# Squares for the RMS norms summed over the channel tiles on VectorE, in place of TensorE

## The chip, the cores and the metric
The kernel runs on one core of a Trainium2 chip. The metric is the device time of one execution, in microseconds (us). Engines are named as the profile names them: PE is TensorE (PEld its weight loads), DVE is VectorE, ACT is ScalarE, POOL is GpSimd, SP is the engine that issues the DMAs.

## What is computed
Two layers of a hybrid block over 512 latent and 256 context tokens of 1024 channels: RMS norm and modulation, one input projection for three branches (attention, a state-space model, a conformer convolution), a gated merge of the branches, an output projection and a gated residual; then a last RMS norm. The norm is what the change touches:

```python
def rmsnorm(x, w):
    xf = x.astype(jnp.float32)
    y = xf * lax.rsqrt(jnp.mean(xf * xf, axis=-1, keepdims=True) + EPS)
    return (y * w.astype(jnp.float32)).astype(x.dtype)
...
    h = rmsnorm(x, norm_w) * (1.0 + scale) + shift
    hc = rmsnorm(xc, norm_w) * (1.0 + scale_c) + shift_c
...
    x_new = x + gate * out
    return x_new, xc + gate_c * out_c
```

The mean is over the 1024 channels of a token. The last layer makes no new context, and its `x_new` goes through the final norm.

## The kernel before
**Layout.** Activations lie channel-major: 8 channel tiles `k` of 128 channels on the partitions, tokens along the free dimension (0 to 511 latent, 512 to 767 context). A sum over channels thus is a sum over 8 tiles and over 128 partitions. Products of float32 are made of three products of shorter parts (`hh`/`hl` or `yh`/`yl` of the data, `whi`/`wlo` of the weights), in `mm_cm_steps` (L161, the product on L175). `wload` (L141) streams weights: a DMA into `raw` (3 buffers), the high part on ACT (L156), the low part on DVE (L157), each with 5 buffers.

**The norm.** `class Rms` (L253) works on a span of tokens in three steps.
- `add` (L261), for each channel tile: ACT squares it into `sq` (L263); then `add_up` has PE multiply `sq` by a 128x32 block of ones (L268), tile `k` into the 32 PSUM partitions of group `k % 4`. After 8 tiles the PSUM tile `ps_ss` holds four partial sums on partitions 0, 32, 64, 96 (and copies beside them). A span over 512 tokens has two such tiles.
- `steps` (L278): ACT copies `ps_ss` to `sspart` (L282); a first yield; PE multiplies `sspart` by `sel4`, which picks the four partitions, 128 tokens to a product (L286), so that tokens come onto the partitions; DVE scales (L288); POOL takes the power −0.5 (L290); a second yield; DVE makes diagonals `dg` (L297), PE spreads them over the partitions with a block of ones into `ps_rb` (L298), ACT copies to `rb` (L299).
- The users: `affine_in` makes `ht` (DVE, L354), `hh` (ACT, L356), `hl` (DVE, L357) of each channel tile; the final norm makes `ot` (DVE, L1138), which goes out by DMA.

Rows of up to 512 tokens (`sq`, `sspart`, `dg`, `rb`, `ht`, and the residual tiles `xr`) share a pool of 7 buffers (tag W2), longer ones a pool of 3 (tag F).

**Where norms stand.** (1) At the start, over all 768 tokens at once, while the modulation weights (`wm`) stream in and PE makes the modulation (`mod_tiles` L221: products L229, ACT copy `part` L232, second step L237, DVE L238); the first products of the conformer, `ps_u`, follow as `hh` comes tile by tile. (2) At the layer boundary, first over the latent span, then over the context span (L382 to L386), while the last tiles of layer 0's output projection `ps_o` run; then come `ps_u` and `ps_g` of layer 1. (3) In the tail, over two parts of 256 latent tokens: 5 output tiles for both parts, then the last 3 for part 1, then the same 3 for part 2, with part 1's norm put between part 2's products. There the order of PE, DVE and ACT is as written (L1155), and `NORM_PACE` says after which pieces of four products (`PIECE` columns) the norm moves on by one yield:

```python
        for ct, w in zip(kept, ws):
            for j, _ in enumerate(out_steps(ct, parts[1:], w)):
                if j == 2:
                    add_up()
                if next(pace):
                    next(first, None)
            add_up = norm_add(1, ct)
```

An output tile (`out_steps`, L1098) fetches `xr` (L1102), makes 24 products per span (`ps_o`, in one of two PSUM banks), and DVE forms `xnew` from `ps_o` and `xr` (L1106), which frees the bank. Apart from the tail, and from PE's order inside a layer, which is as written too, a scheduler orders the instructions of each engine; every engine runs its queue in order.

Of the kernel before, what the change touches and what calls it, by code (L numbers as in the profile page):

```python
# [12 lines left out]
ALU = mybir.AluOpType  # L13
# [28 lines left out]
# How the tensor engine's work is spread, per layer.  # L42
GATES_EARLY = (0, 2)             # tiles of the attention's gate made before the conformer's gate
CONV_GATE_FIRST = (0, 4)         # turns of the conformer's gate before its layer norm
AHEAD_TILES = (1, 3, 5, 7)       # tiles of the last merge whose gates are made ahead of it,
AHEAD = ((2, 3), (3, 4))         # so many by the end of the SSD, and by the end of attention
SSD_END = ((2, 0.5, 2), (2, 0.5, 0))  # turns kept for the SSD's end, its transposes, the first q and k
ATTN_SPARE = (13, 9)             # turns of attention beyond those of its tiles
CTX_TURN = 1.75                  # weight of a turn of a context tile, which has fewer of them
PIECE = 1024                     # columns per piece of woven work  # L50
MOD_LAG = 5120                   # columns between a modulation product and its second step
OUT_FIRST = 3                    # output tiles that take both of their spans at once
KEPT = 3                         # last output tiles, whose weights stay for the second part
NORM_PACE = (0, 0, 1, 0, 0, 1, 0, 0, 0)  # pieces of the last products after which the norm moves on, at first
# [3 lines left out]
def hybrid_kernel(ctx, tc, xT, cc, consts, rope, mod_params, params, fnw, w_mod, w_cm, w_q, w_kvd, w_z,  # L58
# [48 lines left out]
    # ---- inputs that the start waits for  # L107
# [15 lines left out]
    sel, sel4 = cst[:, 384:386], cst[:, 386:388]  # L123
# [8 lines left out]
    def rsqrt(v, scale):  # L132
        """v := (v * scale + eps) ** -0.5"""
        G.tensor_scalar(out=v, in0=v, scalar1=scale, scalar2=EPS, op0=ALU.mult, op1=ALU.add)
        e = nhalf
        for _ in range(len(v.shape) - 2):
            e = e.unsqueeze(1)
        G.tensor_tensor(out=v, in0=v, in1=e.to_broadcast(list(v.shape)), op=ALU.pow)

    def wload(src, nk, ncol, prio=TOP, keep=None):  # L140
        """Stream nk k-tiles of ncol columns, split each into two float32r parts (in keep, where given)."""  # L141
        per, half = {P: (8, 4), 256: (4, 2)}.get(ncol, (2, 2))
        res = []
        with tc.high_priority(offset=prio):
            for k0 in range(0, nk, per):
                n = min(per, nk - k0)
                raw = wp.tile([P, n, ncol], F32, tag="raw", name="raw")
                nc.sync.dma_start(raw, src[:, k0:k0 + n, :])
                for u0 in range(0, n, half):
                    m = min(half, n - u0)  # L150
                    if keep is None:
                        hi = wp.tile([P, m, ncol], F32R, tag="whi", name="whi", bufs=5)
                        lo = wp.tile([P, m, ncol], F32R, tag="wlo", name="wlo", bufs=5)
                    else:
                        hi, lo = (keep[:, i, k0 + u0:k0 + u0 + m, :] for i in range(2))
                    S.activation(hi, raw[:, u0:u0 + m, :], AF.Copy)  # L156
                    V.tensor_tensor(out=lo, in0=raw[:, u0:u0 + m, :], in1=f(hi), op=ALU.subtract)  # L157
                    res += [(hi[:, i, :], lo[:, i, :]) for i in range(m)]
        return res

    def mm_cm_steps(w, xh, xl, ntok, evac, name, col=slice(None), psum=None, late=False, piece=PIECE):  # L161
        """sum_k w[k].T @ x[k] in two parts each, per group of tokens; evac(ps, a, b) takes it.

        Yields the columns streamed, piece by piece, so that the caller can put other work between.
        """
        nk = len(w)
        spans = ntok if isinstance(ntok, tuple) else [(a, min(ntok, a + 512)) for a in range(0, ntok, 512)]
        for a, b in spans:
            ps = (psum or pjt)(name)
            done = 0  # L170
            order = [(k, w[k][i], x) for k in range(nk) for i, x in ((0, xh), (0, xl), (1, xh))]
            if late:
                order.sort(key=lambda o: o[2] is xl)
            for n, (k, st, mv) in enumerate(order):
                T.matmul(ps[:, :b - a], st[:, col], mv(k)[:, a:b], start=(n == 0), stop=(n == len(order) - 1))  # L175
                done += b - a
                if done >= piece and n < len(order) - 1:
                    yield done
                    done = 0
            evac(ps[:, :b - a], a, b)  # L180
            yield done
# [8 lines left out]
    class Weave:  # L190
        """Work of total columns that is emitted piece by piece, spread over n turns of another part."""
# [29 lines left out]
    def mod_tiles(li, mod, m0, tiles, psum=pot):  # L221
        """Columns m0.. of silu(c) @ w_mod + b_mod, channels on partitions; tiles: [P, KD, P] each."""
# [30 lines left out]
    class Rms:  # L253
        """1 / rms over the channels of tokens t0..t1, on every partition; add takes one channel tile."""

        def __init__(self, t0, t1, psum=pot):
            self.t0, self.n, self.psum = t0, t1 - t0, psum
            self.groups = [(a, min(self.n, a + 512)) for a in range(0, self.n, 512)]
            self.pss = [psum("ps_ss") for _ in self.groups]

        def add(self, k, x):  # L261
            sq = row(self.n, "sq")
            S.activation(sq, x[:, self.t0:self.t0 + self.n], AF.Square)  # L263
            g = k % 4

            def add_up():
                for ps, (a, b) in zip(self.pss, self.groups):
                    T.matmul(ps[32 * g:32 * g + 32, :b - a], ones[:, 0:32], sq[:, a:b], start=(k < 4), stop=(k >= 4),  # L268
                             tile_position=(0, 32 * g))
# [8 lines left out]
        def steps(self):  # L278
            n, nt = self.n, self.n // P
            part = row(n, "sspart")  # L280
            for ps, (a, b) in zip(self.pss, self.groups):
                S.activation(part[:, a:b], ps[:, :b - a], AF.Copy)  # L282
            yield
            ps2 = self.psum("ps_ss2")
            for i in range(nt):
                T.matmul(ps2[:, 2 * i:2 * i + 2], part[:, tok(i)], sel4, start=True, stop=True)  # L286
# [31 lines left out]
    for li in range(2):  # L318
# [7 lines left out]
        # ---- per-layer tables  # L326
# [15 lines left out]
        # the attention's scale, a power of two, goes into the weights of the q norm  # L342
# [3 lines left out]
        # ---- norm and modulation  # L346
# [44 lines left out]
        # ---- conformer: gated linear unit, into zero-padded rows that share their pads  # L391
# [7 lines left out]
        # its depthwise convolution is emitted tap by tap  # L399
# [20 lines left out]
        for ct in range(4):  # L420
            # the first products start on channels as the norm hands them over, in banks of their own
# [27 lines left out]
        # ---- k, v, dt (token-major)  # L449
# [13 lines left out]
        # ---- dt = softplus(.), decays  # L463
# [22 lines left out]
        # ---- SSD inputs  # L486
# [51 lines left out]
        # ---- z (token-major)  # L538
# [14 lines left out]
        # ---- decays of the chunks  # L553
# [12 lines left out]
        # ---- q (token-major), kept in DRAM until attention; the conformer's layer norm between its tiles  # L566
# [47 lines left out]
        def gate_steps(c0, c1):  # L614
            """The attention's gate, twice its silu, kept in DRAM until attention's end."""
# [20 lines left out]
        # ---- gated merge of one branch  # L636
        yh, yl = [], []

        def then(fn, steps):
            """The steps, with fn after some of them."""  # L640
# [16 lines left out]
        def ahead_steps(a, b):  # L657
            """Gates of the last merge, kept in DRAM until it."""
# [54 lines left out]
        # ---- SSD states: st[0:4] backward into each latent chunk, st[4:6] forward, rolling  # L713
# [22 lines left out]
        class Chunk:  # L736
            """Output of chunk c, gated and normalised, written over xt[:, c]."""
# [14 lines left out]
            def decay(self, g):  # L752
                """The chunk's own weights, of four heads."""
# [58 lines left out]
        # ---- q / k: norm over the head, rope, transposed and stacked parts  # L812
        def qk_prep(src, nh, t0, nt, wo, cw, sw, dst, dup):
            """src [P, nt, nh*64] token-major (token tiles t0..), into their columns of dst."""
# [47 lines left out]
        class Pipe:  # L862
            """Preparations of q and k, each in three steps, the steps of consecutive ones side by side."""
# [33 lines left out]
        # ---- the SSD's steps, one chunk's decays ahead of another's products  # L897
# [75 lines left out]
        def scores(hp2, qi, fill):  # L973
            """exp(scores - max) over its sum, of two heads for one tile of queries."""
# [79 lines left out]
        # ---- attention, with the merge of the SSD's branch between its steps  # L1054
# [40 lines left out]
        # ---- output projection and residual  # L1095
# [20 lines left out]
        if not last:  # L1116
            # the last tiles' second span comes behind everything else
# [7 lines left out]
    # ---- the last tiles, and the norm, one part of the tokens after another  # L1125
# [29 lines left out]
    # the first part's norm goes between the second part's products  # L1155
# [107 lines left out]
```

## Time and profile before

| what | value |
|---|---|
| runs of the kernel | median 1512.54 us of 3 (1509.86 to 1516.24) |
| span of the profiled execution, first to last instruction | 1508.5 us |
| own time of the profiled execution | not given beside its span |
| PE busy | 1475.4 us (98%) |
| DVE, ACT, POOL busy | 1020.7 (68%), 724.6 (48%), 80.2 us (5%) |
| chain that ended last | PE 93%, DMA 2%, ACT 2%, DVE 1% |
| mean granted TensorE clock | 0.997 |

Busy is the time in which an engine ran instructions; the chain is followed back from the last instruction, at each step to what released it. The median of the runs lies 4.0 us above the profiled span.

### The profile page before, as it was taken

The page shows a single profiled execution, that of the slowest core. Times are in us where ns is not written, and L with a number is a line of the kernel's source. Part 1 is how long each engine was busy: PE and PEld are TensorE (multiplying, and loading weights), DVE is VectorE, ACT ScalarE, POOL GpSimd, SP SyncE. Part 2 cuts the span into 40 slices and gives each one's busy share as a digit, 9 for nine tenths or more (in the row PEclk, how much of TensorE's full clock was granted, in tenths as well). Part 3 has the DMA queues.
Part 4 walks back from the last instruction along what each step waited for, and adds up shares of the span by engine and source line. Part 5 has one row for each costly group of instructions (what it writes and reads, how often), then busy time and mean ns, then how long its engine had stood idle before and what let it go on. Part 6 is the DMA issues. An engine that isn't in the chain of part 4 may idle for free.

```text
span 1508.5 us, 25204 instructions
## 1 busy us (share of the span) xinstructions
PE 1475.4 (98%) x9812; PEld 1257.7 (83%) x9812; DVE 1020.7 (68%) x1876; ACT 724.6 (48%) x1630; POOL 80.2 (5%) x177
## 2 busy tenths in 40 slices
PE   7999999999999999999999999999999999999997
PEld 5898899988888888888888867989988887888886
DVE  3689999666568676555443357899977788665642
ACT  5324543465445575655322254355464657665431
POOL 0000010100003010000000000001010121000000
PEclk9999999999999999999999999999999999999998
DMA  9222333223333323333742422223423242223532
GB/s 377 70 68 92 112 127 100 69 74 105 106 117 128 122 69 123 109 109 107 244 156 91 162 87 80 73 70 113 143 74 112 95 161 71 96 94 105 182 109 74
DMA packets 69687, 172.59 MB, mean 114 GB/s; under 512 B 7872, under 2 KB 24384, under 8 KB 69568
## 3 DMA queue, kind: packets, MB, share of 16 engines
q1 hardware_dynamic: 69568, 170.98, 33.7%
q8 instruction: 77, 1.26, 0.3%
q14 instruction: 42, 0.34, 0.1%
HBM read 143.43 MB, written 27.53 MB: 113 GB/s over the span
## 4 chain that ended last, share of the span: by engine, by line
PE 93%; DMA 2%; ACT 2%; DVE 1%; issue 1%; SPq 0%; POOL 0%; POOLq 0%; DVEq 0%; ACTq 0%
PE ps_gm L175 22%; PE ps_br L175 11%; PE ps_xbc L175 9%; PE ps_o L175 7%; PE ps_u L175 4%; PE ps_gcv L175 4%; PE ps_g L175 4%; PE po_v L1043 3%; PE ps_ga L175 3%; PE pt_p L1029 3%; PE ps_l L983 2%; PE ps_mod L229 2%; PE ps_z L216 1%; PE ps_q L216 1%; PE ps_q L217 1%; PE ps_z L217 1%
## 5 line engine op out<-in xcount | busy, mean ns | idle before, releaser
L156 ACT ACTIVATE whi<-raw 128x512 fp32r<-128x512 f32 (+1 forms) x316 | 199.2, 633 | 291.3 <-PE ps_gm L175 63.9
L157 DVE TENSOR_TENSOR wlo<-raw,whi 128x512 fp32r<-128x512 f32 (+1 forms) x316 | 216.7, 689 | 171.3 <-ACT whi L156 163.1
L175 PE MATMUL ps_gm<-hh,whi 128*128 128x512 f32 (+1 forms) x576 | 212.1, 368 | 0.0
L409 DVE SCALAR_TENSOR_TENSOR vacc<-vt,par,vacc 128x783 f32<-128x783 f32 (+1 forms) x232 | 206.8, 891 | 7.2 <-ACT vacc L406 3.5
L175 PE MATMUL ps_gm<-hh,wlo 128*128 128x512 f32 (+1 forms) x576 | 209.7, 364 | 0.0
L175 PE MATMUL ps_gm<-hl,whi 128*128 128x512 f32 (+1 forms) x576 | 209.2, 363 | 0.0
L175 PEld LDWEIGHTS ps_gm<-hh,whi 128*128 128x128 f32 x576 | 108.8, 189 | 16.3 <-issue 3.1
L175 PEld LDWEIGHTS ps_gm<-hh,wlo 128*128 128x128 f32 x576 | 108.7, 189 | 15.0 <-issue 1.9
L175 PEld LDWEIGHTS ps_gm<-hl,whi 128*128 128x128 f32 x576 | 108.8, 189 | 13.7 <-issue 0.9
L175 PE MATMUL ps_xbc<-hh,whi 128*128 128x512 f32 (+1 forms) x240 | 83.0, 346 | 0.0
L175 PE MATMUL ps_xbc<-hh,wlo 128*128 128x512 f32 (+1 forms) x240 | 82.1, 342 | 0.0
L175 PE MATMUL ps_xbc<-hl,whi 128*128 128x512 f32 (+1 forms) x240 | 82.0, 342 | 0.0
L1035 ACT ACTIVATE pth<-pt_p 128x512 f32<-128x512 f32 x72 | 43.5, 604 | 55.5 <-PE pt_p L1029 55.3
L654 ACT ACTIVATE tg<-ps_gm,hw 128x512 f32<-128x512 f32 x72 | 44.2, 614 | 50.1 <-PE ps_gm L175 50.1
L175 PE MATMUL ps_o<-yl,whi 128*128 128x256 f32 (+1 forms) x208 | 66.5, 320 | 0.0
L175 PE MATMUL ps_o<-yh,whi 128*128 128x256 f32 (+1 forms) x208 | 65.9, 318 | 0.5 <-DVE xnew L1106 0.3
L175 PE MATMUL ps_o<-yh,wlo 128*128 128x256 f32 (+1 forms) x208 | 66.3, 319 | 0.0
L523 DVE SCALAR_TENSOR_TENSOR xacc<-xraw,par,xacc 128x770 f32<-128x770 f32 (+1 forms) x64 | 62.9, 990 | 3.1 <-ACT xacc L520 3.0
L683 DVE SCALAR_TENSOR_TENSOR tg<-tg,ps_br 128x512 f32<-128x512 f32 x66 | 39.6, 599 | 34.9 <-PE ps_br L175 31.0
L1029 PE MATMUL pt_p<-mr,pe 128*128 128x128 f32 x416 | 62.4, 272 | 0.6 <-ACT pth L1035 0.6
L1029 PEld LDWEIGHTS pt_p<-mr,pe 128*128 128x128 f32 x416 | 50.8, 140 | 12.5 <-ACT pth L1035 1.0
L989 DVE TENSOR_REDUCE mx<-ps_l 128x1 f32<-128x512 f32 x64 | 44.0, 689 | 23.2 <-PE ps_l L983 22.5
(278 smaller groups left out, 3670.3 us busy)
## 6 DMA issues: line engine op xcount, KB each, us to landing
raw<-in_w_cm_dram SPq DMA_DIRECT2D x96, 512.0 KB, 3.6
raw<-in_w_mod_dram SPq DMA_DIRECT2D x32, 512.0 KB, 3.6
raw<-in_w_br_dram SPq DMA_DIRECT2D x24, 512.0 KB, 3.6
raw<-in_w_out_dram SPq DMA_DIRECT2D x21, 512.0 KB, 3.7
wm<-in_w_mod_dram SPq DMA_DIRECT2D x16, 512.0 KB, 9.3
ydr<-tg SPq DMA_DIRECT2D x16, 384.0 KB, 4.8
yo<-ydr SPq DMA_DIRECT2D x16, 384.0 KB, 3.4
raw<-in_w_z_dram SPq DMA_DIRECT2D x8, 512.0 KB, 3.8
```

The lines of the kernel that those rows point to most:

```text
L156: S.activation(hi, raw[:, u0:u0 + m, :], AF.Copy)
L157: V.tensor_tensor(out=lo, in0=raw[:, u0:u0 + m, :], in1=f(hi), op=ALU.subtract)
L175: T.matmul(ps[:, :b - a], st[:, col], mv(k)[:, a:b], start=(n == 0), stop=(n == len(order) - 1))
L216: T.matmul(ps[:, :ncol], xh(k)[:, t], hi, start=(k == 0), stop=False)
L409: V.scalar_tensor_tensor(out=acc[:, :n] if j else vt[:, o:o + n], in0=vt[:, o + j:o + j + n], scalar=cw(j), in1=acc[:, :n], op0=ALU.mult, ...
L523: xm = V.scalar_tensor_tensor(out=acc[:, :n], in0=raw[:, j:j + n], scalar=par[:, O_SCW + ct * 5 + j:O_SCW + ct * 5 + j + 1], in1=acc[:, :n ...
L654: lambda ps, a, b: S.activation(tg[:, a:b], ps, AF.Tanh, scale=0.5, bias=hw[:, br * 8 + ct:br * 8 + ct + 1]), "ps_gm")
L683: V.scalar_tensor_tensor(out=tg[:, a:b], in0=tg[:, a:b], scalar=1.0, in1=ps, op0=ALU.add, op1=ALU.mult)
L989: V.tensor_reduce(out=mx[:, 0, j:j + 1], in_=pl[j], axis=AX.X, op=ALU.max, negate=True)
L1029: T.transpose(pt[:, tok(2 * i + j)], pes[j][:, tok(k1 + i)], ident)
L1035: S.activation(pf, pt, AF.Copy)
L1043: T.matmul(po[64 * j:64 * j + 64, 0:P], vv[:, k0 + k1 + i, g, :], pth[:, i, j, :], start=(k1 + i == 0), stop=(k1 + i == nk - 1), tile_posi ...
```

## The change
PE no longer sums over the channel tiles. The first tile's `sq` becomes the accumulator `acc`, and DVE adds every further `sq` to it. PE then multiplies `acc` itself, 128 tokens to a product, by two columns of ones, which sums the 128 partitions and brings tokens onto the partitions as before. The copy to `sspart`, the first yield of `steps` and `sel4` go. (Comments are removed too; line numbers behind the class fall by one.)

```diff
@@ class Rms, __init__
-            self.pss = [psum("ps_ss") for _ in self.groups]
+            self.acc = None
@@ add
             S.activation(sq, x[:, self.t0:self.t0 + self.n], AF.Square)
-            g = k % 4
             def add_up():
-                for ps, (a, b) in zip(self.pss, self.groups):
-                    T.matmul(ps[32 * g:32 * g + 32, :b - a], ones[:, 0:32], sq[:, a:b], start=(k < 4), stop=(k >= 4),
-                             tile_position=(0, 32 * g))
+                if self.acc is None:
+                    self.acc = sq
+                else:
+                    V.tensor_tensor(out=self.acc, in0=self.acc, in1=sq, op=ALU.add)
@@ steps
-            part = row(n, "sspart")
-            for ps, (a, b) in zip(self.pss, self.groups):
-                S.activation(part[:, a:b], ps[:, :b - a], AF.Copy)
-            yield
-            ps2 = self.psum("ps_ss2")
+            ps2 = self.psum("ps_ss")
             for i in range(nt):
-                T.matmul(ps2[:, 2 * i:2 * i + 2], part[:, tok(i)], sel4, start=True, stop=True)
+                T.matmul(ps2[:, 2 * i:2 * i + 2], self.acc[:, tok(i)], ones[:, 0:2], start=True, stop=True)
```

Counted over the program, PE loses 8 products of 512 and 8 of 256 columns at the start, 8 and 8 at the boundary, 16 of 256 in the tail; ACT loses 6 copies; DVE gains 7 adds of 768 elements, 7 of 512, 7 and 14 of 256.

The scheduler moves other instructions with these. At the start, the queue of ACT from the second copy `part` to the first `hh`. Before:

```order
L232 ACTIVATE part<-ps_mod 128x256 x2
L156 ACTIVATE whi<-raw 128x512 x2
L299 ACTIVATE rb<-ps_rb 128x512
L299 ACTIVATE rb<-ps_rb 128x256
L156 ACTIVATE whi<-raw 128x512 x2
L356 ACTIVATE hh<-ht,mod_160 128x512
```

and now:

```order
L232 ACTIVATE part<-ps_mod 128x256
L156 ACTIVATE whi<-raw 128x512 x2
L298 ACTIVATE rb<-ps_rb 128x512
L298 ACTIVATE rb<-ps_rb 128x256
L156 ACTIVATE whi<-raw 128x512
L446 ACT_TABLE_LOAD
L446 ACTIVATE na<-par 128x16
L232 ACTIVATE part<-ps_mod 128x256
L355 ACTIVATE hh<-ht,mod_160 128x512
```

The first `hh` stood behind two weight tiles (four `whi`); now a third tile's `whi`, a table load, `na` (an exponential of a parameter) and a further `part` stand ahead of it. On PE 56 modulation products and three second steps stand ahead of the first `ps_u`, where 48 and two stood.

At the boundary, the queue of DVE where the latent span's norm is finished. Before:

```order
L288 TENSOR_SCALAR rs<-ps_ss_9298 128x4
L297 TENSOR_SCALAR dg<-mr,rs 128x128 x4
L157 TENSOR_TENSOR wlo<-raw,whi 128x512
L1106 SCALAR_TENSOR_TENSOR xnew<-ps_o,mod_160,xr 128x256
L157 TENSOR_TENSOR wlo<-raw,whi 128x512
L354 SCALAR_TENSOR_TENSOR ht<-xnew,aw,rb 128x512
```

and now:

```order
L287 TENSOR_SCALAR rs<-ps_ss 128x4
L1105 SCALAR_TENSOR_TENSOR xnew<-ps_o,mod_160,xr 128x256
L296 TENSOR_SCALAR dg<-mr,rs 128x128 x4
L157 TENSOR_TENSOR wlo<-raw,whi 128x512
L353 SCALAR_TENSOR_TENSOR ht<-xnew,aw,rb 128x512
```

The last `xnew` of the projection moved ahead of the diagonals. On PE 8 products `ps_o` stand between the sum product and `ps_rb`, where 20 stood.

In the tail, the end of DVE's queue, from the scaling of part 1's norm. Before:

```order
L288 TENSOR_SCALAR rs<-ps_ss_15416 128x2
L297 TENSOR_SCALAR dg<-mr,rs 128x128 x2
L1138 SCALAR_TENSOR_TENSOR ot<-xnew,fnw_sb,rb 128x256
L1106 SCALAR_TENSOR_TENSOR xnew<-ps_o,mod_161,xr 128x256
L1138 SCALAR_TENSOR_TENSOR ot<-xnew,fnw_sb,rb 128x256 x6
L1106 SCALAR_TENSOR_TENSOR xnew<-ps_o,mod_161,xr 128x256
L1138 SCALAR_TENSOR_TENSOR ot<-xnew,fnw_sb,rb 128x256
L288 TENSOR_SCALAR rs<-ps_ss_15509 128x2
```

and now:

```order
L287 TENSOR_SCALAR rs<-ps_ss 128x2
L1105 SCALAR_TENSOR_TENSOR xnew<-ps_o,mod_161,xr 128x256
L296 TENSOR_SCALAR dg<-mr,rs 128x128 x2
L272 TENSOR_TENSOR sq<-sq 128x256
L1137 SCALAR_TENSOR_TENSOR ot<-xnew,fnw_sb,rb 128x256 x2
L1105 SCALAR_TENSOR_TENSOR xnew<-ps_o,mod_161,xr 128x256
L1137 SCALAR_TENSOR_TENSOR ot<-xnew,fnw_sb,rb 128x256 x3
L272 TENSOR_TENSOR sq<-sq 128x256
L1137 SCALAR_TENSOR_TENSOR ot<-xnew,fnw_sb,rb 128x256 x3
L1105 SCALAR_TENSOR_TENSOR xnew<-ps_o,mod_161,xr 128x256
```

With one yield less, part 1's norm moves one stop of `NORM_PACE` forward: `rs` now comes before the `xnew` of the tile during which it is made, `dg` after it, and all eight `ot` of part 1 and two adds come before the last `xnew`. On PE 12 products `ps_o` stand between the sum product and `ps_rb` of part 1.

## Rows read from the trace of the kernel before
**Rows 1.** The page, part 4: the chain, share of the span by engine.

```profile
PE 93%; DMA 2%; ACT 2%; DVE 1%; issue 1%; SPq 0%; POOL 0%; POOLq 0%; DVEq 0%; ACTq 0%
```

**Rows 2.** Windows: stretch, length, busy us (instructions) by engine, PEclk, DMA share, GB/s.

```profile
core 0: us, PE busy (x) PEld busy (x) DVE busy (x) ACT busy (x) POOL busy (x), PEclk, DMA share, GB/s
0.00:20.00 20.00, 12.97 (x112) 7.17 (x112) 0.55 (x4) 9.78 (x14) 1.33 (x5) 1.00 0.92 353
...
865.00:885.00 20.00, 20.00 (x107) 12.17 (x106) 6.95 (x11) 9.55 (x16) 0.00 (x0) 1.00 0.33 117
...
1460.00:1480.00 20.00, 20.00 (x148) 17.19 (x147) 2.42 (x5) 2.08 (x5) 0.00 (x0) 1.00 0.13 40
...
1500.00:1508.00 8.00, 1.19 (x4) 0.93 (x4) 3.62 (x10) 0.38 (x1) 0.00 (x0) 0.50 0.40 131
```

**Rows 3.** Timeline, PE, boundary: start, length, engine, line, operation, instructions.

```profile
865.24 0.28 PE L175 MATMUL ps_o<-yl,whi 128*128 128x256 f32 x1
...
866.42 0.38 PE L175 MATMUL ps_o<-yh,wlo 128*128 128x256 f32 x1
866.65 0.28 PE L175 MATMUL ps_o<-yh,whi 128*128 128x256 f32 x1
```

**Rows 4.** Timeline, PE, tail: one output tile and its sum.

```profile
1462.44 0.28 PE L175 MATMUL ps_o<-yh,whi 128*128 128x256 f32 x1
...
1463.42 0.28 PE L175 MATMUL ps_o<-yh,wlo 128*128 128x256 f32 x1
...
1466.02 0.28 PE L175 MATMUL ps_o<-yh,whi 128*128 128x256 f32 x1
```

**Rows 5.** Chain in order of time: sums of the context span, start, length, what.

```profile
898.97 0.55 PE ps_ss L268 x2
...
907.33 0.56 PE ps_ss L268 x4
```

**Rows 6.** Groups by shape, DVE: adds. Busy us, mean ns, idle before.

```profile
L805 DVE TENSOR_TENSOR y<-y,y 128x512 f32<-128x512 f32 x18 | 12.4, 686 | 0.2
...
L789 DVE TENSOR_TENSOR y<-pyd,y 128x256 f32<-128x256 f32 x20 | 8.3, 417 | 2.8 <-PE pyd L786 2.5
```

**Rows 7.** Timeline, the tail's end, PE, DVE and ACT.

```profile
1491.00 0.61 PE L298 MATMUL ps_rb<-dg,cst 128*128 128x128 f32 x4
...
1493.00 2.46 DVE L1138 SCALAR_TENSOR_TENSOR ot<-xnew,fnw_sb,rb 128x256 f32<-128x256 f32 x6
...
1496.71 0.42 ACT L263 ACTIVATE sq<-xnew 128x256 f32<-128x256 f32 x1 [3.11 <-DVE xnew L1106]
...
1498.27 0.61 PE L286 MATMUL ps_ss<-cst,sspart 128*128 128x2 f32 x4 [0.47 <-ACT sspart L282]
```

**Rows 8.** Timeline, boundary, DVE and PE; in brackets idle before, and releaser.

```profile
887.36 0.16 DVE L288 TENSOR_SCALAR rs<-ps_ss 128x4 f32<-128x4 f32 x1
888.64 0.96 DVE L297 TENSOR_SCALAR dg<-mr,rs 128x128 f32<-128x128 f32 x4 [1.12 <-POOL rs L290]
...
892.92 0.50 PE L175 MATMUL ps_u<-hh,whi 128*128 128x512 f32 x1 [2.23 <-ACT hh L356]
...
922.46 0.50 PE L175 MATMUL ps_u<-hh,whi 128*128 128x512 f32 x1 [1.69 <-ACT uu L428]
```

**Rows 9.** Timeline, start, ACT and PE.

```profile
16.32 0.87 ACT L282 ACTIVATE sspart<-ps_ss 128x512 f32<-128x512 f32 x2 [1.53 <-PE ps_ss L268]
...
24.85 0.50 PE L175 MATMUL ps_u<-hh,whi 128*128 128x512 f32 x1
...
26.32 0.62 ACT L156 ACTIVATE whi<-raw 128x512 fp32r<-128x512 f32 x1
26.96 1.28 ACT L447 ACT_TABLE_LOAD   x1
```

**Rows 10.** Waits of PE, 0 to 60 us: in total, times, longest.

```profile
PE ps_u L175 <- ACT hh L356: 1.6, 2, 1.1
...
PE ps_mod L237 <- ACT part L232: 0.6, 1, 0.6
```

**Rows 11.** Waits of DVE, 1443 to 1497 us.

```profile
DVE xnew L1106 <- DMA xr<-xres: 1.3, 1, 1.3
```

More of the change, by code (lines that the diff above doesn't have):

```diff
@@ L122, in hybrid_kernel @@
     m_le, m_ge = cst[:, 128:256], cst[:, 256:384]
-    sel, sel4 = cst[:, 384:386], cst[:, 386:388]
+    sel = cst[:, 384:386]
     S.activation(sc, sc, AF.Silu)
```

## The prediction
> **What bounds the kernel now.** I read the page's chain first: the chain that ended last runs over TensorE (PE) for 93% of the span [rows 1]. So what counts is how much PE work goes, and whether PE then waits for something else. The table by stretches shows that the three places touched differ [rows 2]. From 0 to 20 us the DMA engines are 0.92 busy and PE 13 us of 20: the start waits for data. From 865 to 885 us, the end of layer 0, PE is busy all 20 us and VectorE (DVE) 7. From 1460 to 1480 us PE is full too, and DVE has 2.4 us, ScalarE (ACT) 2.1: the tail is PE alone. The sums of squares ("PE ps_ss L268") are pieces of that chain, so PE's time for them isn't hidden there [rows 5].
>
> **Prices.** One sum over 512 tokens: of three products at 865.24, 866.42 and 866.65 the first two have a sum between them, and the pair takes 1.41 us [rows 3]. Ordinary products of 256 columns start 0.118 apart (22 steps from 1463.42 to 1466.02), so two steps would be 0.24, and the sum costs PE **1.17 us**. Over 256 tokens: from 1462.44 to 1466.02 lie 24 products and one sum, 3.58 − 24 × 0.118 = **0.74 us** [rows 4]. An add on DVE of the same shape has rows elsewhere: 0.69 us for 512 elements, 0.42 for 256 [rows 6].
>
> **The tail.** 15 of the 16 sums stand between ps_o products: 15 × 0.74 = 11.1 us off PE. DVE gets 14 adds of 0.42, 5.9 us, where it has 2.4 us of 20 busy [rows 2]: hidden. An add comes behind its square (0.42 us on ACT), 0.9 us after xnew, while a tile of 24 products lasts 2.8, so the next xnew isn't late; without that cover each would cost 0.8 (rival C). What comes back: with the copy's stop gone, the sum product stands in the middle of the tile over which part 1's norm runs, and rb at that tile's end, 12 products later; on DVE xnew stands between rs and dg. xnew waits for the tile's end, its pitch and a first dg take about 0.45 and 0.24 (a dg is a quarter of 0.96 [rows 8]), and PE starts 0.1 later: it stands 0.8 us at rb. Before, rb came later and waited for nothing. The end: the last square starts at 1496.71 and ends at 1497.13, the second sum starts at 1498.27 [rows 7], with a sum and a copy between: 1.14 us. An add between them makes that about 0.5: −0.6. But the last xnew now stands behind six ot and an add on DVE (six ot took 2.46 [rows 7]) and starts some 0.4 late: net −0.2. Tail: −11.1 + 0.8 − 0.2 = **−10.5**.
>
> **The layer boundary.** Latent span: 8 × 1.17 = 9.4 us off PE. DVE gets 7 adds of 0.69 where it has 7 of 20 us busy: hidden behind PE, as ACT and DVE split weights ahead of it. rb then stands 8 products (0.94 us) behind the sum, where 20 stood (2.4 us). From rs at 887.36 to the first dg's end, 888.64 + 0.24, it took 1.5 us [rows 8], and xnew now lies before dg: PE waits about 0.8 us. The 2.23 us that PE waits for the first hh [rows 8] stay. Context span: its 8 sums lie in five groups, 0.56 us each in the chain, the first and the last in [rows 5]; by the 0.74 of the tail five are 3.7 us off PE. But ht, hh and hl of the norm run beside PE there, 7 adds of 0.42 join them on DVE, and the first ps_u of the next tile waited 1.69 us for uu at 922.46 [rows 8], which ACT makes behind the context span's hh. PE that comes sooner waits longer there, so I count −0.6 of it, between +0.3 (adds in the way) and −3.7 (all kept). Boundary: −9.4 + 0.8 − 0.6 = **−9.2**.
>
> **The start.** 16 sums go from PE, but PE waits for data there; 7 adds on DVE, 0.96 for 768 elements by the slope of [rows 6], fall where DVE has 0.6 us of work [rows 2]. The sums could be ready sooner by a copy (0.87 [rows 9]) and the last square's two sums (1.17 + 0.74), less one add: 1.8, the bound on this side. Against it speaks ACT's new order: the first hh now comes behind the split of the third weight tile, a table load of 1.28 us, a small exponential (na) and a copy (part). That split stood at 26.32, and its data came not long before [rows 9]. With the data at 25.6 to 26.3, 0.62 for the split, 1.28, and 0.6 for na and part, hh starts at 28.1 to 28.8, and the first ps_u 0.8 later, about 29 against 24.85: 4.2 late. PE then waits less afterwards: its waits of 1.6 us for hh and 0.6 for part [rows 10] are used up, and one modulation tile more (0.8 us with its second step) has been done ahead of ps_u. 4.2 − 2.1 − 0.8 = **+1.3**; bounds −1.8 and +4.2.
>
> [...]
>
> **Sum.** +1.3 − 9.2 − 10.5 = −18.4 us on the profiled execution, span 1508.5 to 1490.1. The median of the runs shown, 1512.54, is 4.0 above that span, so I forecast 1512.5 − 18.4 = **1494**. High gain: −1.8 at the start, −13.1 at the boundary and −11.3 in the tail with no stall at rb: −26.2, 1486. Low gain: +4.2, −8.3 and, with rival A, −6: −10, 1502.
>
> **Rivals.**
> *A. PE's freed time in the tail turns into waits for weights and residual tiles (xr).* For: DVE waited 1.3 us for an xr once already [rows 11], the accumulators hold two of the seven buffers from which xr is taken, and PE now asks faster. Against: DMA share 0.13 from 1460 to 1480 [rows 2]. Three or four such waits cost 4 to 5 us: 1498 to 1502.
> *B. The start isn't made good*, the 4.2 us stay (2.9 more than in the sum), and perhaps the clock falls there: at half the clock products take twice as long, by the rb products, so each us of them costs another; I take 0 to 3. 1497 to 1500.
> *C. Slower: the adds hold back DVE's queue.* An add waits in order for its square; behind it stand xnew, which frees one of ps_o's two banks, and the weights' splits. If each square and add is waited out, the price is 0.63 + 0.69 = 1.3 us for 512 tokens and 0.42 + 0.42 = 0.84 for 256: 7 × 1.3 + 21 × 0.84 = 26.7 us, over the 24.2 removed (9.4 + 3.7 + 11.1). With the start at +4.2 the kernel is 7 us slower, 1519. It decides once DVE has more than a tile of PE, 2.8 us, to do per tile; at 7 of 20 and 2.4 of 20 us busy [rows 2] it is far from that.
> *D. More comes back:* the start uses its earlier sums, the context span keeps its 3.7: 1486 to 1489.
> That the sums were hidden anyway is excluded by the chain [rows 5].
>
> **Chances.** Forecast's case 0.50 (1490 to 1497), A 0.17, B 0.15, D 0.12, C 0.06. A measurement of this kernel can tell about 0.5%, 7.6 us, from no change, so faster ends at 1505. The forecast, B, D and nearly all of A lie below that; a deeper A and a mild C lie within, a full C above: faster 0.89, same 0.07, slower 0.04. The range of 1485 to 1502 takes in A to D but for C and the tails of A and D, some 0.15.
>
> **What the new profile would show.** Right: no sums of 512 or 256 columns on PE; ps_o steps of 0.118 throughout the tail, and a wait of 0.8 us for dg at rb; at the boundary one such wait and a longer one for uu; the first ps_u at about 29 us. Wrong: PE waiting for xnew or whi in the tail, DVE for sq with xnew behind it (C); xnew waiting for xr more than once (A); a granted clock of 0.50 after 25 us, or PE waits between 30 and 55 us as long as before although it began late (B); the first ps_u before 26 us (D).

## The result and the profile after

The changed kernel takes 1496.1 us (median of 4 runs, 1495.5 to 1499.5) against 1511.5 of the kernel before beside it: 0.990 of its time, 95% interval 0.988 to 0.991. The forecast was 1494, from 1485 to 1502. Of the forecast's 18.4 us, 15.4 came between the medians and 14.7 between the two profiled spans; the forecast's time looks closer than that because the median that it started from, 1512.5, lies 1.1 above the one measured beside the change. The profiled execution's span went from 1508.5 to 1493.8 us. The page's first line and its chain, after:

```profile
PE 1450.1 (97%) x9716; PEld 1255.5 (84%) x9716; DVE 1039.1 (70%) x1911; ACT 721.9 (48%) x1624; POOL 81.6 (5%) x177
...
PE 91%; DMA 2%; DVE 2%; ACT 2%; issue 1%; SPq 0%; POOL 0%; POOLq 0%; DVEq 0%; ACTq 0%
```

PE is busy for 25.3 us less, 1450.1 against 1475.4, and the span fell by 14.7: the other 10.6 us are new idle time of PE. Of it 7.2 lie before 20 us, where PE gave up work that it had done while waiting for data; most of the rest lies at the boundary and in the tail. Work at half the clock counts as busy (from 27.6 to 31.0 us below, at 0.50, PE is busy 3.40 us of 3.40), so it isn't in the 10.6. The windows of the new trace, to be held against [rows 2]; the columns are the same:

```profile
0.00:20.00 20.00, 5.74 (x68) 5.12 (x72) 7.22 (x11) 9.49 (x14) 1.51 (x5) 1.00 0.92 352
...
27.60:31.00 3.40, 3.40 (x24) 2.65 (x19) 3.37 (x8) 1.28 (x3) 0.00 (x0) 0.50 1.03 411
863.00:883.00 20.00, 19.14 (x148) 18.34 (x147) 15.28 (x30) 11.47 (x19) 1.53 (x11) 1.00 0.53 167
...
915.10:918.40 3.30, 3.30 (x9) 2.53 (x9) 3.30 (x7) 1.99 (x4) 0.00 (x0) 0.50 0.02 8
1239.40:1242.70 3.30, 3.30 (x10) 2.53 (x9) 2.25 (x5) 0.72 (x2) 0.00 (x0) 0.50 0.01 3
1460.00:1480.00 20.00, 19.12 (x160) 18.71 (x159) 7.44 (x20) 3.20 (x8) 0.69 (x1) 1.00 0.15 43
```

At the start PE is busy 5.7 us of 20 instead of 13.0. At the boundary DVE is busy 15.3 us of 20, where it had 7.0, but mostly because PE gets through the stretch sooner (up to the same products, 28 us from 863 us on, DVE had 12.0 before); PE still has 19.1. In the tail PE is no longer full. And there are three stretches at a granted clock of 0.50 in the midst of PE's work (low stretches, below), none of which the first trace had.

**Where the time went.** The products are the same in both traces, so the start of each can be subtracted, which gives its offset: a ps_u that began at 922.46 [rows 8] begins at 913.89, 8.57 us early. Taken at the ends of the three places, and for the experiments below too (us, minus is earlier than the first profile of before; "first" is the third modulation product, at 14.0 us of before, whose weights a transfer brings; "start" is the further slip up to 60 us, "boundary" from 850 to 940 us, "tail" from 1440 us to the last rb, "elsewhere" the rest):

| execution | first | start | boundary | tail | elsewhere | all |
|---|---|---|---|---|---|---|
| the change | −0.5 | +2.4 | −8.1 | −8.8 | +0.3 | −14.8 |
| the change, c2 | +0.6 | +2.2 | −7.0 | −8.2 | +0.2 | −12.2 |
| the change, f3 | −0.7 | +4.9 | −6.8 | −8.9 | +0.1 | −11.4 |
| before, c1 | +1.9 | +0.2 | 0.0 | 0.0 | 0.0 | +2.1 |
| e1, start as before | −0.5 | +2.1 | −8.0 | −9.1 | +3.3 | −12.2 |
| e2, tail only | −0.3 | +1.9 | +0.9 | −7.8 | −0.4 | −5.7 |
| e3, boundary only | +0.2 | −0.1 | −8.0 | −0.4 | +3.6 | −4.7 |
| e4, sums kept at the start | +1.2 | +5.2 | −9.5 | −8.7 | +1.6 | −10.2 |
| e5, pace | −0.7 | +1.6 | −8.0 | −9.9 | −1.3 | −18.3 |
| e6, accumulators apart | +0.7 | +1.1 | −8.0 | −9.5 | −1.3 | −17.1 |
| e7, own bank | +0.3 | +4.3 | −9.3 | −8.1 | +1.9 | −10.8 |
| f1, pace, start as before | +0.7 | +0.1 | −8.0 | −10.5 | +3.8 | −13.9 |
| f2, pace again | −0.7 | +1.4 | −8.0 | −9.9 | −1.7 | −18.8 |

The three executions of the change agree within 0.7 us in the tail, within 1.3 at the boundary, where their clocks differ, and worst at the start, from +2.2 to +4.9.

**What PE waits for now.** At the boundary (860 to 930 us) and in the tail (1430 to 1490 us), the view of waits: in total, times, longest.

```profile
PE ps_u L175 <- ACT hh L355: 3.2, 3, 2.2
PE ps_u L175 <- ACT uu L427: 2.5, 1, 2.5
PE ps_rb L297 <- DVE dg L296: 0.9, 1, 0.9
...
PE ps_rb L297 <- DVE dg L296: 2.2, 2, 1.4
PE ps_ss L285 <- DVE sq L272: 1.7, 1, 1.7
PE ps_o L175 <- DVE xnew L1105: 1.4, 2, 1.0
```

The wait for uu grew from 1.69 [rows 8] to 2.50; that for dg at rb is new in both places, as forecast (in the tail the longest, 1.4, is the end's, the other 0.8 is part 1's). PE waits 1.4 us for xnew in the tail, once 1.0. The timeline of DVE there:

```profile
1448.03 1.29 DVE L157 TENSOR_TENSOR kept<-raw,kept 128x512 fp32r<-128x512 f32 x2 [1.97 <-ACT kept L156]
1450.17 0.48 DVE L1105 SCALAR_TENSOR_TENSOR xnew<-ps_o,mod,xr 128x256 f32<-128x256 f32 x1 [0.84 <-DMA xr<-xres]
```

DVE's queue stands first for a weight tile's split and then for xr.

### The profile page after: what moved, and what is told of

Read it like the earlier page. It is cut to its first block, busy times and chain, and to the rows that moved or that the text cites. A ratio compares the mean times of both kernels' runs of the same rounds, so it can differ in the third digit from the quotient of the medians.

```text
span 1493.8 us, 25061 instructions
## 1 busy us (share of the span) xinstructions
PE 1450.1 (97%) x9716; PEld 1255.5 (84%) x9716; DVE 1039.1 (70%) x1911; ACT 721.9 (48%) x1624; POOL 81.6 (5%) x177
## 4 chain that ended last, share of the span: by engine, by line
PE 91%; DMA 2%; DVE 2%; ACT 2%; issue 1%; SPq 0%; POOL 0%; POOLq 0%; DVEq 0%; ACTq 0%
PE ps_gm L175 23%; PE ps_br L175 11%; PE ps_xbc L175 9%; PE ps_o L175 6%; PE ps_gcv L175 4%; PE ps_g L175 4%; PE ps_u L175 4%; PE po_v L1042 3%; PE ps_ga L175 3%; PE pt_p L1028 3%; PE ps_l L982 2%; PE ps_mod L229 2%; PE ps_z L216 1%; PE ps_q L216 1%; PE ps_q L217 1%; PE ps_z L217 1%
## 5 line engine op out<-in xcount | busy, mean ns | idle before, releaser
L1028 PEld LDWEIGHTS pt_p<-mr,pe 128*128 128x128 f32 x416 | 50.9, 140 | 11.7 <-issue 0.2
```

The source lines that it names most:

```text
L1028: T.transpose(pt[:, tok(2 * i + j)], pes[j][:, tok(k1 + i)], ident)
```

## The experiments

All kernels but the controls c1, c2, f3 have both forms of the norm's class, the old one (`Rms`) and the changed one (`RmsV`), and choose at each place.

**e1, the start as before.**

```diff
-                rb0 = rms_bcast(xk, 0, NT, RmsV)
+                rb0 = rms_bcast(xk, 0, NT, Rms)
```

> Boundary and tail changed, start as before. Theory (each place acts for itself, the start is a loss): products behind the start stand where they stood before the change, within 0.1 us, instead of 1.87 us later, with the granted clock at 1.00 from 20 to 40 us; against before the time falls by 1.9 us more than the whole change, some 17 us (ratio 0.989 to 0.988). Rival (the sums on PE at the start cost time too, and the change wins there once nothing else is in the way): no better than the whole change, and products at 52 us as late as with it.

Measured: 1496.6 us, ratio 0.990 (0.988 to 0.992), no better than the change. But the rival isn't shown by that either: the products at 60 us came 1.7 us late with a program that up to there has the order of the kernel before on every engine. The clock was at 0.50 from 20.4 to 27.2 us in this execution, and again at 887, 915, 1017 and 1242 us. The theory's forecast of the clock was wrong; e3 and f1, with the same start and no low stretch in it, show the start at −0.1 and +0.1.

**e2, only the tail, and e3, only the boundary.** `Rms` at the two other places.

> Only the tail changed. Theory: until 1440 us nothing moves (offset 0 within 0.2 us, and no granted clock of 0.50 before the end); from the first ps_o of the tail to the end PE gains 11.1 us of sums and loses 1.3 us where an xnew is held up and 1.0 us at rb: 8.8 us less than before, ratio 0.994. Rival (the tail's gain depended on PE coming early from the boundary, or on noise): 11 us or more, or under 6 us.

> Only the layer boundary changed. Theory: no offset before 865 us, PE gains 9.4 us in the latent span, gives 1 to 2 us back at rb and ends the boundary (first product of the conformer's second tile) 8 to 10 us early; 7 to 10 us less than before, ratio 0.994 to 0.995. If the clock falls again around the wait for uu and in attention, by 1.4 and 1.6 us, the gain is 6 to 7. Rival (adds in DVE's queue hold PE there): under 5 us, with PE waiting for xnew between 865 and 885 us.

Measured: e2 0.995 (0.993 to 0.996), tail −7.8; e3 0.996 (0.994 to 0.998), boundary −8.0, with −9.5 of it up to 922 us and 1.6 given back at the low clock behind it. The two ratios add to 0.990, the change's own: two places make up the gain, each for itself, and neither rival holds. What e2 was expected to show before 1440 us failed: it is the kernel before up to there, and yet it lost 1.9 us at the start and 0.9 at the boundary, and its windows show

```profile
24.40:27.80 3.40, 3.40 (x23) 2.68 (x24) 3.40 (x9) 3.38 (x7) 0.00 (x0) 0.50 1.03 407
894.80:898.10 3.30, 3.30 (x9) 2.60 (x8) 3.30 (x6) 2.65 (x5) 0.00 (x0) 0.50 0.00 0
```

so a low stretch alone is no mark of the change.

**e4, the old sums kept at the start, unread.** `add_up` issues the old PE products too.

```diff
             def add_up():
+                for ps, (a, b) in zip(self.pss, self.groups):
+                    T.matmul(ps[32 * g:32 * g + 32, :b - a], ones[:, 0:32], sq[:, a:b], start=(k < 4), stop=(k >= 4),
+                             tile_position=(0, 32 * g))
                 if self.acc is None:
```

> The whole change, but at the start PE also makes the old sums, which nobody reads. Theory A (the clock falls at the start because PE stands idle just before the first ps_u): PE waits as long before the first ps_u at 28 to 29 us, so the granted clock is 0.50 there again, and products at 52 us are 1.5 to 2.5 us late as with the change. Theory B (it falls because PE has too little to do in the first 20 us without the sums): the clock stays at 1.00 from 20 to 40 us and products at 52 us are at most 0.5 us late.

Measured: 1499.8 us, 0.993 (0.991 to 0.994). The windows, and PE's wait in them:

```profile
0.00:20.00 20.00, 12.13 (x93) 5.97 (x94) 7.31 (x11) 9.90 (x14) 0.19 (x4) 1.00 0.93 354
...
23.90:30.60 6.70, 6.43 (x44) 5.57 (x48) 3.20 (x11) 3.77 (x7) 0.00 (x0) 0.50 1.03 408
...
PE ps_mod L229 <- DMA wm<-in_w_mod_dram: 2.7, 1, 2.7
```

PE is busy 12.1 us of the first 20, near the 13.0 of before, and the clock falls all the same, at the end of 2.7 us of waiting for a transfer. So theory B fails for this later fall. Theory A isn't shown either: the place was another (PE waited before the modulation products, and the clock was at 1.00 again when the first ps_u began at 31.4 us), and the products at 52 us came 4.1 us late, not 1.5 to 2.5. B has a point in something else: the sums bring the clock up sooner. The trace's own record of the clock begins with its first change, a rise to 1.00: at 10.1 to 14.0 us in the seven profiled executions that have the sums on PE at the start, at 20.8 to 34.1 us in the seven that don't. The 12 products that sum the partitions, in the timeline of PE (start, us, what), take here

```profile
19.00 1.48 PE L336 MATMUL ps_ss<-cst,sq 128*128 128x2 f32 x12
```

and in the change

```profile
15.35 2.72 PE L285 MATMUL ps_ss<-cst,sq 128*128 128x2 f32 x12 [0.80 <-DVE sq L272]
```

But here the sums didn't hold the clock through the 2.7 us of waiting for wm. In this kernel ACT also makes rb behind the table load, and the clock was low again from 54.6 to 61.4 us, so that its slip of 5.2 us isn't the change's.

**c1 and c2, the two kernels again.**

> The kernel before, once more. What the first profiles left open: the stretches at a granted clock of 0.50. If they come by chance in both kernels, this execution shows one or two of them before the end (the first profile of before had none, and the tail-only kernel, which is the kernel before up to 1440 us, had two, at 24 and 895 us), and its span is above 1508.5 by some 1.6 us for each. If the change makes them, there is none here, and the span is 1508 to 1509.

> The changed kernel, once more. If the low stretches come by chance, they lie in part elsewhere than at 27.6, 915 and 1239 us and number one to four; with each taken off at what the products in it lose (about 1.6 us, less where PE waits anyway) the span comes to 1489 to 1490. If they belong to the change, the same three are there, and the span is 1493 to 1495. Boundary (865 to 922 us of before, up to the second ps_u tile) 9.6 us gained in either case, tail 8 to 9.

Measured: c1 has no low stretch, its span 1510.6 is longer by the 2 us that its first transfers came later. c2 has low stretches at 29, 886, 916 and 1241 us, and f3 (below) at 887, 918 and 1242. So neither expectation holds whole: a low stretch comes by chance at the start, but those of 914 to 918 us and of 1239 to 1242 us were there in all three executions of the changed kernel that have a profile, and in neither of the kernel before.

**e5, the tail's first yield put back.**

```diff
         def steps(self):
             n, nt = self.n, self.n // P
+            if self.first:
+                yield
```

> The whole change, with the first yield of the norm's steps put back, in the tail only: the sum product stands one stop later, rb behind half of the next tile. Theory (PE waits at rb because xnew stands between rs and dg and there are only 12 products to cover it): the wait of 0.8 us for dg at part 1's rb is gone and the 1.0 to 1.1 us that PE loses there; from the first ps_o of the tail to the last rb PE gains 9.9 to 10 us against before, instead of 8.9. Rival (PE would wait there for something else just after, such as a bank or ot): the gain stays under 9.2.

Measured: tail −9.9 instead of −8.2 to −8.9; one execution of 1491.8 us. PE's waits in its tail:

```profile
PE ps_o L175 <- DVE xnew L1156: 2.1, 2, 1.7
PE ps_ss L336 <- DVE sq L326: 1.8, 1, 1.8
PE ps_rb L348 <- DVE dg L347: 1.4, 1, 1.4
```

The wait for dg is down from two to the one of the end: the theory of that stall holds. Taken by itself, from 1485.0 to 1491.7 us of before, the place is clear in every profile: the eight executions with the changed tail and without the yield lose 1.4 us there, e5 and the two below that have the yield (f1, f2) lose nothing. That the whole tail meets the forecast of 9.9 is in part luck: 1.4 us came back instead of 1.0 to 1.1, and xnew at 1459 us cost 1.9 instead of 1.3.

**e6, the tail's accumulators in another pool.**

```diff
-            sq = row(self.n, "sq")
+            if self.own and k == 0:
+                sq = fill([P, self.n], "acc")
+            else:
+                sq = row(self.n, "sq")
```

> The whole change, with the tail's two accumulators in the pool of long rows, so that all seven short rows are left for squares and residual tiles. Theory (PE stands about 1.3 us at 1459 us of before's time because xr comes late for want of a buffer): no wait of xnew for xr, and that loss goes or falls under 0.4; the tail gains 9.7 to 10.2 us. Rival (xnew is late there because it stands on DVE behind weight splits that wait for their transfer): the loss stays at 0.9 to 1.5 and the tail's gain at 8 to 9.2.

Measured: tail −9.5, PE's wait for xnew 1.2 us. DVE's waits in the tail:

```profile
DVE kept L157 <- ACT kept L156: 4.7, 2, 2.7
...
DVE xnew L1156 <- DMA xr<-xres: 0.9, 1, 0.9
```

xnew still waits for xr, by 0.9 us, and PE loses 1.1 us there, within the 1.0 to 2.3 of the executions without this edit: a buffer more doesn't remove the wait. On SP's queue the xr transfers stand behind two weight transfers, and in the kernel before xnew waited 1.3 us for the same transfer [rows 11] without holding up PE. Neither expectation holds whole: the loss is the rival's, the tail of −9.5 lies between the two. What an earlier issue of xr would bring is not tested.

**e7, a bank of its own for the second tile.**

```diff
-            if li == 0 and ct == 1:
+            if ct == 1:
```

> The whole change; in layer 1 the products of the conformer's second tile get PSUM banks of their own, as layer 0 gives them already. Theory (with the sums gone PE reaches the second tile before its bank is free, stands 2.5 us for the copy uu, and the low stretch of the clock at 914 us comes from standing there): no wait of PE for uu, the clock at 1.00 from 900 to 930 us, and the products at 926 us of before stand 9 to 12 us early instead of the change's 7.8 to 8.2 after its own start; 2 to 3.5 us faster than the change. Rival (the context span's hh on ACT and DVE is what PE waits for, whichever bank): PE waits as long for hh a little later, the low stretch stays, and less than 1 us is gained.

Measured: 1498.5 us, 0.991 (0.990 to 0.993). PE's waits at the boundary, and the window behind it:

```profile
PE ps_u L175 <- ACT hh L406: 2.4, 2, 2.2
PE ps_g L175 <- ACT tgl L484: 1.7, 1, 1.7
PE ps_rb L348 <- DVE dg L347: 0.9, 1, 0.9
...
900.00:930.00 30.00, 28.28 (x127) 22.84 (x126) 22.07 (x43) 14.13 (x27) 1.30 (x7) 1.00 0.24 77
```

The wait for uu is gone and no low stretch follows, and the boundary gains 1.3 us more, though a low stretch from 887 to 894 us fell in it. This is one profile; e4 waited 2.1 us for uu and drew no low stretch there either. But 0.9 us went again at 1000 to 1040 us, where the orders of ACT and DVE have changed too, and the start was 4.3 us late: the 2 to 3.5 us forecast for the whole did not come.

**f1, f2, f3, timed together.** f1 is e5 with the start as before, f2 is e5 again, f3 the changed kernel again.

> The start as before, boundary changed, tail changed with the first yield put back. Theory (the start's new order costs 1.1 to 1.6 us, the tail's stop 1.0 to 1.3, the rest is as in the change): start 0, boundary 8.0 us gained after its low stretch, tail 9.5 to 9.9: 2 to 3 us faster than the change, 17 to 19 under before. Rival (how many low stretches an execution draws decides, at 0.8 to 1.6 us each, and the start is within that): no faster than the change by the interval, medians within 1.5 us of each other.

> The whole change with the first yield put back in the tail, timed. Theory: 1.0 to 1.4 us faster than the change; part 1's rb without a wait of PE. Rival: within 0.5 us of it, the loss moved to another place of the tail.

> The changed kernel, timed beside the two others on the same chip. Theory: 15 to 16 us under before (1.0%), with a low stretch near 914 us in its profile as in every kernel whose boundary was changed and whose second tile had no bank of its own.

Measured: f1 1495.8 us, 0.989 (0.988 to 0.991); f2 1491.9 us, 0.987 (0.986 to 0.989); f3 1495.6 us, 0.988 (0.987 to 0.990), 16.3 us under before, with its low stretch at 918 us; that every such kernel has one isn't so, as e4 has none. f2 is the best kernel of the study by its median, 1.3% under the kernel before; over the changed kernel the times don't prove it, as the intervals meet, but the tail does: −9.9 in both executions against −8.2 to −8.9 in three. f1's start cost nothing (+0.1), but it lost 4 us near 1017 and 1242 us, where its clock was low. Of them 0.9 at 1017 are lost in e3 and e7 too, without the low clock; f1's orders of ACT and DVE near there differ from the change's as well. So f1's rival is right that the start's gain doesn't show in the whole, and the clock accounts for the larger part of why.

## Why the prediction was right, point by point

**Start, +1.3 forecast.** Right in kind and, where the clock let it, in size. ACT and PE of the change:

```profile
24.44 0.63 ACT L156 ACTIVATE whi<-raw 128x512 fp32r<-128x512 f32 x1 [0.69 <-DMA raw<-in_w_cm_dram]
25.08 1.28 ACT L446 ACT_TABLE_LOAD   x1
...
26.76 2.12 ACT L355 ACTIVATE hh<-ht,mod 128x512 fp32r<-128x512 f32 x4
...
26.92 0.61 PE L237 MATMUL ps_mod<-cst,part 128*128 128x2 f32 x4 [2.27 <-ACT part L232]
...
28.40 0.80 PE L175 MATMUL ps_u<-hh,whi 128*128 128x512 f32 x1
28.99 0.63 PE L175 MATMUL ps_u<-hh,wlo 128*128 128x512 f32 x1
```

The first hh stands behind the third tile's split, the table load and a copy, as the order said; the transfer came 1.2 us or more sooner than I took, and the first ps_u began at 28.4, 3.6 us late instead of 4.2. It then lost more: 28.40 to 28.99 are 0.59 us between two products that were 0.34 apart before, and the window from 27.6 on shows the clock of 0.50. Behind it PE had no wait left but one of 1.1 us, and by 60 us +2.4 was left. With full pace there (e5, f2, e6) it is +1.1 to +1.6. No run changes ACT's order alone, so what the table load and the copy cost by themselves is read from these rows and not tested. Rival B's second half thus happened, in this execution and in four of the seven others with the new start, where the clock fell there or came up late (c2, f3, e7, e4; not in e5, f2, e6). That the clock could fall there was a guess of mine: the trace of before shows no fall ahead of 1499.9 us, and the sum has no term for one. The rb products that B goes by are those of the end, four in 1.19 us from 1500.31 on, at a PEclk of 0.50 [rows 2], against four in 0.61 at 1491.00 [rows 7], where it was 1.00. For B's 0 to 3 us the runs showed 0.8 to 1.9 us for a low stretch where PE had work throughout. The first rise of the clock came at 20.8 us or later without the sums on PE and at 14.0 us or sooner with them. The fall behind it isn't the change's alone, since e1 and e2 show one with the old start. In the change and c2, where the clock rose at 21 and 22 us, PE then waited 2.3 and 2.2 us for part and the clock fell behind it; in e5, f2 and e6, where it rose at 25.5 to 26.6 us, PE came to part later, waited 0.5 us, and the clock stayed.

**Boundary, −9.2 forecast.** −8.1, and the terms can be told apart. Behind the last ps_o the offset was −8.25 from +1.11: 9.4, as from [rows 3]. At rb PE lost 1.1 instead of 0.8; the row of DVE shows xnew between rs and dg, as the order said, and a weight's transfer ahead of it:

```profile
880.53 0.16 DVE L287 TENSOR_SCALAR rs<-ps_ss 128x4 f32<-128x4 f32 x1
881.58 0.48 DVE L1105 SCALAR_TENSOR_TENSOR xnew<-ps_o,mod,xr 128x256 f32<-128x256 f32 x1 [0.89 <-DMA raw<-in_w_cm_dram]
881.98 0.87 DVE L296 TENSOR_SCALAR dg<-mr,rs 128x128 f32<-128x128 f32 x4
```

(The releaser named is what came last by the profile; xnew also waits for its ps_o, and I don't settle which it was.) The context span gained 1.4 up to 922 us instead of 0.6, from −7.15 to −8.57. That is −9.7 in all. Then the clock fell at 915, behind the 2.5 us for uu, and took 1.6 of it: −8.57 became −7.01. That is the part that the prediction had nowhere: it forecast a longer wait for uu and priced it as the wait alone.

**Tail, −10.5 forecast.** −8.8; this term was too large. The sums gave what [rows 4] said: offsets fall by 0.74 to 0.75 at each, from −8.37 to −9.12 at the first behind 1460 us. The stall at rb was 0.8 us of waiting, as worked out, but 1.4 of offset: past rb, from 1485.0 to 1491.7 us of before, two sums are gone and the offset gains 0.1 instead of 1.5. The 0.6 beyond the wait stay unexplained. The end gained 0.4 instead of 0.2. What the sum lacked most is 1.3 us at 1459 us of before's time, where xnew came late; it is rival A's mechanism, at one place and of a third of its price. It varied from 1.0 to 2.3 us between executions.

**Elsewhere, 0 forecast.** +0.3, made of −0.8 and −0.5 (near 675 and 1023 us, where the offset changes without any change of the program's PE order) and +1.6 at the low stretch of 1239 us. The −0.8 looks like lateness of the start made good: e1, with the old start and +2.1 there, gains 0.7 at the same place, and e3, which was on time, nothing. The prediction had no term for it, and so had luck by 1.3 us.

**The sum and the rivals.** −18.4 was forecast for the profile and −14.7 came. The 3.7 between them are made of 3.2 at the two low stretches of 915 and 1239 us, 1.7 in the tail (1.3 at xnew and 0.6 at rb, less 0.2 at the end) and 1.1 at the start, 6.0 together; against them stand 0.5 that the boundary gained over its term up to 922 us, 0.5 of the first transfer and the 1.3 of the two places elsewhere. In e5 and f2, which drew no low stretch at 1240 us and none at the start, −18.3 and −18.8 stand although one at 914 us is in both; but these have the yield back and so no stall at rb, and don't show that the change alone would reach the forecast. Rival C, the adds that hold DVE, has a small part. In the tail it didn't happen: DVE waited 5.9 us there for squares, with 7.4 of 20 us busy. At the boundary the chain that ended last, in order of time (start, us, what), does run over DVE, from the first add to rb; between the first two rows it alternates adds with splits of weights:

```profile
870.89 0.69 DVE sq L272
...
877.80 3.78 DMA raw<-in_w_cm_dram
881.59 0.28 DVE xnew L1105
...
881.98 0.29 DVE dg L296
```

It names the engine whose work ended last, and PE had no wait for xnew from 863 to 880 us; so DVE's queue can have cost what rb took beyond the 0.8 forecast, 0.3 us, and hardly more. Rival D didn't happen.

## What to carry to other kernels

Where PE fills its stretch, a product moved to an engine with room is worth its full time on PE (here 9.4 us for eight sums of 512 columns at the boundary, and 0.74 to 0.75 for each of 256 in the tail), and that time is read from the start-to-start steps of its neighbours; what comes back has to be looked for in the queues' new order (a yield less moved xnew between rs and dg, which putting it back undid) and in every wait that PE now meets earlier (that for uu grew from 1.69 to 2.50 us). A wait on PE is to be priced with the clock behind it as well: behind those 2.50 us the low stretch took another 1.6. Where single executions differ by more than the question, subtract the starts of equal products from two traces, place by place, rather than compare medians.

## What the runs showed of the hardware

The granted clock fell to 0.50 in the midst of work, in the change at 27.6, 915.0 and 1239.3 us, after waits of PE of 2.3, of 2.5 and, in two pieces, of 1.0 us. At the boundary the products run like this, at a step of 0.23 and then of 0.43 us:

```profile
914.70 0.39 PE L175 MATMUL ps_u<-hh,whi 128*128 128x512 f32 x1
914.93 0.52 PE L175 MATMUL ps_u<-hl,whi 128*128 128x512 f32 x1
915.24 0.63 PE L175 MATMUL ps_u<-hh,wlo 128*128 128x512 f32 x1
915.67 0.63 PE L175 MATMUL ps_u<-hh,whi 128*128 128x512 f32 x1
```

PE had waited 2.5 us up to 913.89 and worked again for 1.2 us when the clock fell. The kernel before waited 1.69 us at the same place and didn't lose the clock there in either profile; e3's wait of 2.08 us was followed by it, e4's of the same length wasn't. A wait of two microseconds isn't needed either: before the fall at 1239 us PE had waited in the last 12 us only for these two, up to 1236.8 and 1238.7 us (in total, times, longest):

```profile
PE pt_qk L857 <- ACT kk L858: 0.6, 1, 0.6
PE ps_l L982 <- ACT qt L858: 0.4, 1, 0.4
```

Whether the same program loses the clock at a given place also differs between executions: at 886 us c2 and f3 did and the first execution of the change didn't, and at 1240 us three of three executions of the change did while e5, e6 and f2, which have the same order on PE, DVE and ACT up to the tail, didn't. A low stretch cost 0.8 to 1.9 us where PE had work throughout. What decides between two equal executions stays open.

In two executions (f3, e7) the first ps_u products were 0.59 us apart, as at half the clock, while PEclk stood at 1.00 from 20 to 40 us. The 12 products that make rb at the start, in the change and in f3:

```profile
21.19 1.58 PE L297 MATMUL ps_rb<-dg,cst 128*128 128x128 f32 x12
...
21.52 2.91 PE L297 MATMUL ps_rb<-dg,cst 128*128 128x128 f32 x12
```

The change's 12 sum products of 2.72 us (under e4), 1.50 in the kernel before, stand under a PEclk of 1.00 too. The clock's record begins at 20.8 us in the change, at 33.9 in f3 and at 34.1 in e7, and the column shows 1.00 for the time before it. At the very start of an execution it therefore doesn't tell, also not in [rows 2] for the first 11.7 us, up to which the kernel before has no record; the steps of the products do.
